# RWKV-7 and forgetting attention on one core: recurrence units of two chunks of four head pairs, and a gate made by a dense stream

## The chip, the cores and the metric

One core of one Trainium2 chip runs the whole forward pass as one program. The metric is the time of that program on the device in microseconds (us). The engines are TensorE (PE in the profile; PEld is its weight load), VectorE (DVE), ScalarE (ACT), GpSimd (POOL) and SyncE (SP), which here issues all DMAs.

## What is computed

A trunk of two layers over 1024 tokens of width 1024, 16 heads of 64, all float32. The first layer is RWKV-7 time mixing, the second forgetting attention; each is followed by a squared-ReLU MLP. The change touches time mixing only:

```python
xr, xw, xk, xv, xa, xg = (h + xx * mu[j] for j in range(6))
r, k, v = xr @ wr, xk @ wk, xv @ wv
w_log = -softplus(-(w0 + tanh(xw @ w1) @ w2)) - 0.5
a = sigmoid(a0 + (xa @ a1) @ a2)
g = sigmoid(xg @ g1) @ g2                      # (T,160) @ (160,1024)
...
sa = einsum('bhvk,bhk->bhv', S, a_t)           # one step of the state, head by head
S = S * w_t[:, :, None, :] + sa[..., :, None] * b_t[..., None, :] + v_t[..., :, None] * k_t[..., None, :]
y = einsum('bhvk,bhk->bhv', S, r_t)
...
y = groupnorm(y) * ln_w + ln_b + bonus
x = x + (1 + gate) * ((y * g) @ wo)
```

## The kernel before

**Chunks and units.** The recurrence is done in chunks of 64 tokens. Two heads lie on the 128 partitions and make a head pair; there are 8 pairs (p in the code) and 16 chunks. A unit (u, 16 of them) is two pairs by four chunks, 256 tokens of one half of the sequence (j): `where(u)` names them, units 0 to 7 are the first half. For each unit `early` makes the decays, scales keys and queries (`ar`, `bk`), and inverts 16x16 blocks on VectorE (L772, L773, through DRAM `Ld`, `T16d`); `late` makes the in-chunk products (`sc`, `xk`, `tt`, `uv`, `bkt`); `chain` carries the state; `gate` normalises the result, multiplies it by the gate and stores it to `yd`.

**A step of the chain.** For each chunk c: state times `ar` into the PSUM tile `pq`, and the state's part of the read-out into `py` (both by `both`, L875); VectorE adds (`xs`, L892); `tt` times `xs` (L875); ScalarE and VectorE copy it into `uv` (L898, L899); for each pair `bkt` times `uv` (L906) and VectorE's state update (L910), GpSimd having scaled the old state (`sp`, L867); and the rest of the read-out (L915). `pq` is one PSUM bank with one buffer. Each `yield` of `chain` ends an inner step, three a chunk.

**What sets the order.** `units` writes the chain's steps at high priority; after each, `step` takes a number of pieces from three other generators in NR rounds: the preparation of later units (PR a step), the gate of the last unit (NG, or NG8 in unit 8), and `beside`, the dense stream (NA, NC or NB a step by the unit). `issue_after` holds these behind the step's instructions, and a scheduler then fixes each engine's order. A piece of the dense stream is one weight tile's share of three f32r matmuls of 128x512 (`mm3`, L124, L126, L128: high by high, low input by high weight, high input by low weight). The dense stream is: the rest of the first half's `v`, then the second half's low-rank projections, `r`, `k`, `v` and the gate's first product (`lora_g`), then, once eight units are gated (`ngated`), the output projection and the MLP of the first half. Ahead of the units, `rest` drains the first half's `r` and `lora_g` beside `early` of units 0 and 1, and `done` takes N0 pieces of `v`.

**The gate.** `lora_g` stores 128 of the 160 sigmoid rows to `gad` in DRAM and keeps 32 in `zt`. `gate` loads them and, for each of the unit's two pairs, the two parts of `g2`, and makes the gate by two fp32 matmuls of 256 columns (L943, L944) into one PSUM tile, by which VectorE multiplies (L946). In the trace an fp32 matmul is two instructions.

## Time and profile before

| what | us |
|---|---|
| median of three runs (3390.83 to 3399.28) | 3394.84 |
| the profiled execution | 3394.05 |
| its span, first to last instruction | 3392.1 |
| opening, to the first state matmul | about 333 |
| recurrence, to the last state matmul | about 1304 |

The profile is of one execution. Busy times are sums over an engine's instructions; a matmul's listed duration includes its way through the array, so consecutive ones overlap and a share near 100% doesn't say how closely they follow each other. A window is a stretch of the span; a wait is idle time of an engine put down to what ended it. In a timeline the first number is the start, and the spacing of starts is what one instruction takes of the queue's time.

### The profile page before, as it was taken

The page shows a single profiled execution, that of the slowest core. Times are in us where ns is not written, and L with a number is a line of the kernel's source. Part 1 is how long each engine was busy: PE and PEld are TensorE (multiplying, and loading weights), DVE is VectorE, ACT ScalarE, POOL GpSimd, SP SyncE. Part 2 cuts the span into 40 slices and gives each one's busy share as a digit, 9 for nine tenths or more (in the row PEclk, how much of TensorE's full clock was granted, in tenths as well). Part 3 has the DMA queues.
Part 4 walks back from the last instruction along what each step waited for, and adds up shares of the span by engine and source line. Part 5 has one row for each costly group of instructions (what it writes and reads, how often), then busy time and mean ns, then how long its engine had stood idle before and what let it go on. Part 6 is the DMA issues. An engine that isn't in the chain of part 4 may idle for free.

```text
span 3392.1 us, 50350 instructions
## 1 busy us (share of the span) xinstructions
PE 3214.4 (95%) x19108; PEld 2438.4 (72%) x19108; DVE 1943.0 (57%) x3239; ACT 1432.8 (42%) x2284; POOL 1358.7 (40%) x868
## 2 busy tenths in 40 slices
PE   4898999999999999899999999999999999999997
PEld 2456666666777776678887777777778888778886
DVE  7496765766556534167786433555566666454344
ACT  3642236523433223242233556667555544332323
POOL 3364432333333233354444432444423333454444
PEclk7899999899999999899999999999999999999999
DMA  7374344355333223236752233666544443232222
GB/s 276 98 234 151 95 128 135 116 152 150 88 102 102 85 76 125 68 111 224 229 187 88 85 131 119 207 203 182 177 128 136 144 134 100 88 111 95 98 98 83
DMA packets 294065, 452.90 MB, mean 134 GB/s; under 512 B 114720, under 2 KB 170432, under 8 KB 293824
## 3 DMA queue, kind: packets, MB, share of 16 engines
q1 hardware_dynamic: 293824, 449.68, 42.3%
q8 instruction: 152, 2.49, 0.3%
q14 instruction: 89, 0.73, 0.1%
HBM read 371.25 MB, written 78.32 MB: 133 GB/s over the span
## 4 chain that ended last, share of the span: by engine, by line
PE 50%; DVE 4%; ACT 2%; DMA 1%; issue 1%; POOL 1%; SPq 0%; DVEq 0%; ACTq 0%; POOLq 0%
PE pj L124 8%; PE pj L128 7%; PE pj L126 7%; PE pk L128 7%; PE pk L124 7%; PE pk L126 7%; PE pt L1328 2%; PE po L1313 1%; PE po L1314 1%; PE ps L1285 1%; PE ps L1286 1%; DVE t L239 1%; DVE hl L241 1%; DVE x L1016 1%; DVE modacc L185 0%
## 5 line engine op out<-in xcount | busy, mean ns | idle before, releaser
L117 POOL TENSOR_TENSOR wl<-wraw,wh 128x1024 fp32r<-128x1024 f32 x385 | 947.7, 2462 | 1231.7 <-ACT wh L116 1162.6
L116 ACT CAST wh<-wraw 128x1024 fp32r<-128x1024 f32 x385 | 402.6, 1046 | 822.0 <-PE pk L126 359.2
L124 PE MATMUL pj<-hh,wh 128*128 128x512 f32 x1120 | 448.6, 408 | 7.4 <-DVE sq L1090 2.7
L128 PE MATMUL pj<-hh,wl 128*128 128x512 f32 x1120 | 445.1, 403 | 5.5 <-POOL wl L117 5.5
L126 PE MATMUL pj<-hl,wh 128*128 128x512 f32 x1120 | 443.2, 401 | 0.0
L1016 DVE SCALAR_TENSOR_TENSOR x<-pj,G,x 128x512 f32<-128x512 f32 x304 | 225.8, 747 | 164.3 <-PE pj L128 162.2
L128 PE MATMUL pk<-hh,wl 128*128 128x512 f32 x688 | 272.1, 402 | 8.6 <-POOL wl L117 8.6
L124 PE MATMUL pk<-hh,wh 128*128 128x512 f32 x688 | 270.2, 398 | 8.9 <-ACT wh L116 7.8
L126 PE MATMUL pk<-hl,wh 128*128 128x512 f32 x688 | 267.3, 395 | 0.0
L124 PEld LDWEIGHTS pj<-hh,wh 128*128 128x128 f32 x1120 | 210.9, 189 | 61.9 <-issue 4.5
L1016 DVE SCALAR_TENSOR_TENSOR x<-pk,G,x 128x512 f32<-128x512 f32 x240 | 176.2, 746 | 135.7 <-PE pk L128 135.2
L128 PEld LDWEIGHTS pj<-hh,wl 128*128 128x128 f32 x1120 | 210.6, 188 | 58.9 <-POOL wl L117 7.7
L126 PEld LDWEIGHTS pj<-hl,wh 128*128 128x128 f32 x1120 | 211.1, 189 | 48.1 <-issue 2.4
L124 PE MATMUL pj<-mh,wh 128*128 128x512 f32 x564 | 236.9, 421 | 6.0 <-DVE mr L1046 3.0
L126 PE MATMUL pj<-ml,wh 128*128 128x512 f32 x564 | 224.3, 398 | 0.0
L128 PE MATMUL pj<-mh,wl 128*128 128x512 f32 x564 | 219.4, 399 | 2.4 <-POOL wl L117 2.4
L124 PE MATMUL pk<-mh,wh 128*128 128x512 f32 x460 | 182.1, 398 | 8.9 <-DVE mr L1046 5.4
L166 ACT CAST mh<-mr 128x512 fp32r<-128x512 f32 x128 | 79.5, 621 | 250.6 <-PE pj L128 109.1
L126 PE MATMUL pk<-ml,wh 128*128 128x512 f32 x460 | 181.7, 395 | 0.0
L185 DVE SCALAR_TENSOR_TENSOR modacc<-modw,cact,modacc 128x1024 f32<-128x1024 f32 x98 | 155.1, 1583 | 31.0 <-DMA modw<-in_modw_dram 22.5
L128 PE MATMUL pk<-mh,wl 128*128 128x512 f32 x460 | 166.6, 397 | 0.0
L124 PEld LDWEIGHTS pk<-hh,wh 128*128 128x128 f32 x688 | 130.7, 190 | 42.8 <-ACT wh L116 11.6
(334 smaller groups left out, 6493.2 us busy)
## 6 DMA issues: line engine op xcount, KB each, us to landing
wraw<-in_up_dram SPq DMA_DIRECT2D x128, 512.0 KB
wraw<-in_down_dram SPq DMA_DIRECT2D x128, 512.0 KB
modw<-in_modw_dram SPq DMA_DIRECT2D x96, 512.0 KB
wraw<-in_wqg_dram SPq DMA_DIRECT2D x32, 512.0 KB
wraw<-in_wk_dram SPq DMA_DIRECT2D x24, 512.0 KB
wraw<-in_wv_dram SPq DMA_DIRECT2D x24, 512.0 KB
x<-in_xT_dram SPq DMA_DIRECT2D x32, 256.0 KB
wraw<-in_wr_dram SPq DMA_DIRECT2D x16, 512.0 KB
```

Of the source, the lines that this page charges most:

```text
L116: nc.scalar.copy(out=wh, in_=raw)
L117: self.weng.tensor_tensor(out=wl, in0=raw, in1=wh.bitcast(F32), op=ALU.subtract)
L124: mm(out=p, lhsT=wh, rhs=hh[k], start=first, stop=False)
L126: mm(out=p, lhsT=wh, rhs=hl[k], start=False, stop=False)
L128: mm(out=p, lhsT=wl, rhs=hh[k], start=False, stop=last)
L166: self.nc.scalar.copy(out=out_h, in_=src)
L185: nc.vector.scalar_tensor_tensor(out=acc, in0=w, scalar=ck, in1=acc, op0=ALU.mult, op1=ALU.add)
L239: nc.vector.scalar_tensor_tensor(out=t, in0=x[k], scalar=A[:, k:k + 1], in1=rs, op0=ALU.mult, op1=ALU.mult)
L241: nc.vector.scalar_tensor_tensor(out=hl[k], in0=t, scalar=sh[:, k:k + 1], in1=hh[k].bitcast(F32), op0=ALU.add, op1=ALU.subtract)
L1016: self.nc.vector.scalar_tensor_tensor(out=x[j][m], in0=ps, scalar=gain[:, m:m + 1], in1=x[j][m], op0=ALU.mult, op1=ALU.add)
L1285: PE.matmul(out=o[:, 0:r], lhsT=qs[:, q], rhs=kh[:, i * n:i * n + r], start=True, stop=False)
L1328: PE.transpose(out=pt[:, i * 256 + b * 128:i * 256 + (b + 1) * 128], in_=Ps[b][:, (k + i) * 128:(k + i + 1) * 128], identity=ident)
```

## The change

A unit becomes four pairs by two chunks (128 tokens). Each inner step so works on four pairs, and there are half as many; the numbers of pieces a step are about doubled (NR 8, NA 5, NC 6, NB 10.8, PR 3.6, NG 4, NG8 1.6). The state tiles are 128x256 instead of 128x128, the decay takes four matmuls of 128 columns instead of two of 256, and loads that go by pair are four instead of two. The state matmuls of a chunk are held behind the preceding read-out's, and the read-out's rest behind the state update's. `x2` reuses `x1`'s memory. `lora_g` now stores all 160 rows; a new generator `gates` reads a half's rows back, splits them and `g2` into high and low parts, and makes the gate for all 8 pairs by dense f32r matmuls: three with K of 128 and one with K of 96 that carries the three products of the 32-row remainder. The result goes to DRAM (`gd`); `gate` loads its part, and GpSimd multiplies. `gates` stands in the dense stream, for the first half at its head, for the second at the end. The second half's `v` runs beside `lora_g`. The opening takes 33 pieces of `r` and of `v` where it took 17.

```diff
-    N0 = 17
-    NR = 4
+    N0 = 33
+    NR = 8
-    NA = 2.2
+    NA = 5
-    NB = 5.4
-    NC = 3
+    NB = 10.8
+    NC = 6
-    PR = 2.2
-    NG = 2
+    PR = 3.6
+    NG = 4
...
         def dense():
+            yield from self.gates(0, ev)
             yield from v
             yield from self.lora_wa(h, 1, lw, al)
-            for i in (1, 2, 0):
+            for i in (1, 2):
                 yield from self.stream(h, 1, i, xj, ev, al)
-            yield from self.lora_g(h, 1, lw)
+            yield from self.both(self.lora_g(h, 1, lw), self.stream(h, 1, 0, xj, ev, al), 2)
+            yield from self.gates(1, ev)
...
+    def gates(self, j, ev):
+        nc, S, V = self.nc, self.nc.scalar, self.nc.vector
+        s = slice(j * HT, (j + 1) * HT)
+        f = lambda n, d=F32R, b=1: ev.tile([128, HT], d, name=n, tag=n, bufs=b)
+        gh, gl, gr = f("e2"), f("e3"), f("e1", F32R, 2)
+        g, r = self.t(), self.t()
+        nc.sync.dma_start(out=g, in_=self.gad[0:128, s])
+        self.split(gh, gl, g)
+        nc.sync.dma_start(out=r[0:32], in_=self.gad[128:160, s])
+        S.copy(out=gr[0:32], in_=r[0:32])
+        S.copy(out=gr[64:96], in_=r[0:32])
+        V.tensor_tensor(out=gr[32:64], in0=r[0:32], in1=gr[0:32].bitcast(F32), op=ALU.subtract)
+        wh, wl = self.load_w(self.ap["g2"][:, 0:128].rearrange("m k n -> k m n"))
...
+        for m in range(KT):
+            p = self.bank()
+            self.mm3([p], wh[:, m], wl[:, m], [(j, [gh], [gl])], 0, True, False)
+            nc.tensor.matmul(out=p, lhsT=wr[0:96, m], rhs=gr[0:96], start=False, stop=True)
+            yield
+            o = f("e0", F32, 2)
+            S.copy(out=o, in_=p)
+            nc.sync.dma_start(out=self.gd[m][:, s], in_=o)
...
         C = 8
+        Q, N = 4, 2
-            j, g, q = u // 8, u % 8 // 2, u % 2
-            return j, 2 * g, slice(j * HT + q * 256, j * HT + (q + 1) * 256)
+            j, g, q = u // 8, u % 8 // 4, u % 4
+            return j, Q * g, slice(j * HT + q * 128, j * HT + (q + 1) * 128)
...
-            for c in range(4):
+            for c in range(N):
...
-                    for q in range(2):
-                        ins = both(ps[:, q], ar[:, 0, q * 4 + c], st[:, q], True, True)
+                    with ExitStack() as ea:
+                        if ins is not None:
+                            ea.enter_context(tc.issue_after(ins.ins))
+                        for q in range(Q):
+                            ins = both(ps[:, q], ar[:, 0, q * N + c], st[:, q], True, True)
...
-                for q in range(2):
-                    for e in range(2):
-                        ins = PE.matmul(out=ys[q][H[e]], lhsT=uv[:, q * 4 + c, e], rhs=sc[:, q * 4 + c, e, 1], start=first and q == 0, stop=c + q == 4)
+                with tc.issue_after(ins.ins):
+                    for q in range(Q):
+                        for e in range(2):
+                            ins = PE.matmul(out=ys[q][H[e]], lhsT=uv[:, q * N + c, e], rhs=sc[:, q * N + c, e, 1], start=first and q == 0, stop=c == N - 1 and q == Q - 1)
...
-            ga = lng("ga", [128, 256], 1)
-            nc.sync.dma_start(out=ga, in_=self.gad[:, ts])
+            g = lng("g", [128, W], 1)
+            nc.sync.dma_start(out=two(g), in_=pair(self.gd, p, ts))
...
-                PE.matmul(out=ps[:, c], lhsT=g2[:, 0], rhs=ga, start=True, stop=False)
-                PE.matmul(out=ps[:, c], lhsT=g2[96:128, 1], rhs=self.zt[96:128, ts], start=False, stop=True)
-                yield
-            V.tensor_tensor(out=y, in0=y, in1=ps, op=ALU.mult)
+            yield
+            G.tensor_tensor(out=y, in0=y, in1=g, op=ALU.mult)
```

How this stands on TensorE, in the order that the program fixes. In these rows `pj` with `wh` or `wl` is a dense matmul, and a count xn is of matmuls as written.

Before, in unit 1: a chain block, one piece of the gate (L943, L944) and dense work.

```order
L906 MATMUL pq<-uv,bkt 64x64
L875 MATMUL py<-ar,st 64x64
L906 MATMUL pq<-uv,bkt 64x64
L875 MATMUL py<-ar,st 64x64
L943 MATMUL pms<-ga,g_2999 128x256
L944 MATMUL pms<-zt,g_2999 128x256
L715 MATMUL pe<-ar,bk 64x64 x8
L126 MATMUL pj<-xl,wh 128x512
L128 MATMUL pj<-xh,wl 128x512
L124 MATMUL pj<-xh,wh 128x512
L126 MATMUL pj<-xl,wh 128x512
L128 MATMUL pj<-xh,wl 128x512
```

State update (L906) and read-out (L875) alternate one by one, and the gate's two fp32 matmuls follow on the same queue.

After, in unit 8: the gate's columns of the second half (`e` is the split gate input, L614 the matmul with K of 96) between preparation and state updates of two matmuls.

```order
L944 MATMUL pq<-uv,bkt 64x64 x2
L749 MATMUL pl<-dT_2018,x_6966 64x64
L614 MATMUL pj<-e_6937,wh 128x512 x2
L749 MATMUL pl<-ta,lb 32x32 x16
L944 MATMUL pq<-uv,bkt 64x64 x2
L124 MATMUL pj<-e_6935,wh 128x512
L126 MATMUL pj<-e_6936,wh 128x512
L128 MATMUL pj<-e_6935,wl 128x512
L614 MATMUL pj<-e_6937,wh 128x512
L124 MATMUL pj<-e_6935,wh 128x512
L126 MATMUL pj<-e_6936,wh 128x512
L128 MATMUL pj<-e_6935,wl 128x512
```

The gate of all pairs is now dense work; the fp32 gate matmuls stand nowhere.

After, in unit 8, some 40 rows on: the end of its first chunk and the first two steps of its second.

```order
L833 MATMUL pl<-ar,bk 128x128 x4
L944 MATMUL pq<-uv,bkt 64x64 x4
L954 MATMUL py<-sc,uv 64x64 x8
L909 MATMUL py<-ar,st 64x64 x6
L749 MATMUL pe<-ar,bk 64x64
L909 MATMUL pq<-st,ar 64x64 x8
L909 MATMUL py<-ar,st 64x64 x2
L749 MATMUL pe<-ar,bk 64x64 x15
L124 MATMUL pj<-hh,wh 128x512
L909 MATMUL pq<-xs,tt 64x64 x8
L126 MATMUL pj<-hl,wh 128x512
```

The read-out and the state products stand in blocks of six to eight matmuls; from the last gate column to the `hh` matmul (the output projection's first) there is no dense work in this step.

Before, the first state matmul of all (L875, `pq<-sc,tt`) and the rows ahead of it, dense matmuls of the stream `v`:

```order
L126 MATMUL pj<-xl,wh 128x512
L128 MATMUL pj<-xh,wl 128x512
L124 MATMUL pj<-xh,wh 128x512
L126 MATMUL pj<-xl,wh 128x512
L128 MATMUL pj<-xh,wl 128x512
L875 MATMUL pq<-sc,tt 64x64 x4
L604 MATMUL pms<-cs,e_2280 128x128 x4
```

After, the same place:

```order
L749 MATMUL pl<-tt,x_2231 32x32 x16
L871 MATMUL pl<-sg,cs 128x512
L124 MATMUL pj<-e_2055,wh 128x512
L126 MATMUL pj<-e_2056,wh 128x512
L128 MATMUL pj<-e_2055,wl 128x512
L614 MATMUL pj<-e_2057,wh 128x512
L909 MATMUL pq<-sc,tt 64x64 x8
L880 MATMUL pl<-cs,bk 128x128 x4
```

The dense matmuls ahead of it are now the gate's of the first half. In all 570 dense matmuls stood ahead of the first state matmul, and now 520, 16 of them the gate's.

## Rows read from the trace of the kernel before

**Rows 1.** The page's part 1, whole execution: busy us (share) xinstructions.

```profile
PE 3214.4 (95%) x19108; PEld 2438.4 (72%) x19108; DVE 1943.0 (57%) x3239; ACT 1432.8 (42%) x2284; POOL 1358.7 (40%) x868
```

**Rows 2.** Windows: stretch, length, busy us (xinstructions) by engine, granted clock, DMA share, GB/s.

```profile
0.00:330.00 330.00, 253.85 (x1093) 157.67 (x1094) 225.97 (x297) 135.99 (x187) 154.38 (x111) 0.84 0.57 189
330.00:1304.00 974.00, 949.33 (x8626) 664.94 (x8626) 572.28 (x1273) 361.05 (x563) 335.57 (x269) 0.98 0.38 112
```

**Rows 3.** Waits of TensorE, 330 to 1304 us: total us, times, longest.

```profile
PE pj L126 <- DVE xl L167: 8.0, 4, 4.5
PE pq L875 <- DVE st L910: 3.9, 2, 2.9
PE pj L124 <- DVE x L1016: 2.9, 4, 1.5
```

**Rows 4.** Windows: a stretch of unit 10 without dense matmuls.

```profile
884.00:897.00 13.00, 9.28 (x162) 6.86 (x158) 6.77 (x15) 5.60 (x9) 2.21 (x3) 0.84 0.33 98
```

**Rows 5.** Timeline of TensorE: start us, us, line, operation; a gate piece in unit 1.

```profile
438.39 0.70 PE L943 MATMUL pms<-ga,g 128*128 128x256 f32 x2
439.02 0.69 PE L944 MATMUL pms<-zt,g 32*128 32x256 f32 x2
439.64 0.49 PE L799 MATMUL pl<-ar,bk 64*128 64x128 f32 x2
440.06 0.50 PE L124 MATMUL pj<-xh,wh 128*128 128x512 f32 x1
440.39 0.40 PE L126 MATMUL pj<-xl,wh 128*128 128x512 f32 x1
```

**Rows 6.** Timeline of TensorE: ten dense matmuls, then a short block.

```profile
424.67 0.39 PE L126 MATMUL pj<-xl,wh 128*128 128x512 f32 x1
...
427.00 0.40 PE L128 MATMUL pj<-xh,wl 128*128 128x512 f32 x1
427.32 0.33 PE L915 MATMUL py<-sc,uv 128*64 128x64 f32 x2
```

**Rows 7.** Timeline of TensorE: chain blocks, in fours, woven, and alternating.

```profile
431.08 0.34 PE L906 MATMUL pq<-uv,bkt 128*64 128x64 f32 x4
431.35 0.50 PE L128 MATMUL pj<-xh,wl 128*128 128x512 f32 x1
...
436.35 0.27 PE L915 MATMUL py<-sc,uv 128*64 128x64 f32 x1
436.36 0.27 PE L906 MATMUL pq<-uv,bkt 128*64 128x64 f32 x1
...
436.86 0.50 PE L124 MATMUL pj<-xh,wh 128*128 128x512 f32 x1
...
440.95 0.33 PE L906 MATMUL pq<-uv,bkt 128*64 128x64 f32 x2
441.21 0.33 PE L875 MATMUL py<-ar,st 64*64 64x64 f32 x2
441.46 0.33 PE L906 MATMUL pq<-uv,bkt 128*64 128x64 f32 x2
```

**Rows 8.** Timeline of TensorE: transposes, then the decay matmuls of a unit.

```profile
431.69 1.03 PE L846 MATMUL pl<-cs,bk 128*128 128x128 f32 x8
432.65 0.45 PE L875 MATMUL pq<-sc,tt 64*64 64x64 f32 x8
433.03 1.13 PE L737 MATMUL pe<-zt,w 65*128 65x256 f32 x4
434.00 1.02 PE L931 MATMUL pms<-t,blk_m 128*128 128x512 f32 x2
```

**Rows 9.** Windows: the end of the opening.

```profile
170.00:285.00 115.00, 98.06 (x414) 63.48 (x414) 108.00 (x129) 42.63 (x62) 74.53 (x44) 0.91 0.63 208
285.00:333.00 48.00, 47.60 (x388) 36.12 (x388) 20.24 (x51) 10.34 (x16) 15.20 (x11) 0.96 0.50 148
```

**Rows 10.** Groups of VectorE, 330 to 1304 us: busy us, mean ns, idle before.

```profile
L910 DVE SCALAR_TENSOR_TENSOR st<-pq,pc,sp 128x64 f32<-128x64 f32 x88 | 24.6, 279 | 46.3 <-PE pq L906 45.6
```

More of the change, by code (lines that the diff above doesn't have):

```diff
@@ L372, in run @@
                 self.take(m1, 100)
-                rs = self.rs = [xq.tile([128, HT], F32, name=f"rs{j}") for j in range(2)]
+                rs = self.rs = [xq1.tile([128, HT], F32, name=f"rs{j}") for j in range(2)]
                 self.rms(x[0], rs[0])
@@ L524, in phase_rwkv @@
         else:
-            self.take(r, 17)
+            self.take(r, 33)
         v = self.stream(h, 0, 0, xj, ev, al)
@@ L585, in lora_g @@
-        nc.sync.dma_start(out=self.gad[:, s], in_=g)
+        for p, o, n in ((ps[0], 0, 128), (ps[1], 128, 32)):
+            g = self.t()
+            S.activation(out=g[0:n], in_=p[0:n], func=AF.Tanh, scale=0.5)
+            nc.gpsimd.tensor_scalar(out=g[0:n], in0=g[0:n], scalar1=0.5, scalar2=0.5, op0=ALU.mult, op1=ALU.add)
+            nc.sync.dma_start(out=self.gad[o:o + n, s], in_=g[0:n])
+    def gates(self, j, ev):
[11 more added lines that the diff above has]
+        wh, wl = self.load_w(self.ap["g2"][:, 0:128].rearrange("m k n -> k m n"))
+        raw, wr = (self.wp.tile([128, KT, 128], d, name=n, tag=n, bufs=b) for n, d, b in (("wraw", F32, self.NW[0]), ("wh", F32R, self.NW[1])))
+        for i in range(3):
+            nc.sync.dma_start(out=raw[i * 32:(i + 1) * 32], in_=self.ap["g2"][:, 128:160].rearrange("m k n -> k m n"))
+        S.copy(out=wr[0:96], in_=raw[0:96])
+        self.weng.tensor_tensor(out=wr[64:96], in0=raw[64:96], in1=wr[64:96].bitcast(F32), op=ALU.subtract)
+        for m in range(KT):
[6 more added lines that the diff above has]
+            nc.sync.dma_start(out=self.gd[m][:, s], in_=o)
@@ L735, in early @@
             ps = bank("pe")
-            for q in range(2):
-                PE.matmul(out=ps[:, q * 256:(q + 1) * 256], lhsT=w2[:, q], rhs=self.zt[0:65, ts], start=True, stop=True)
+            for q in range(Q):
+                PE.matmul(out=ps[:, q * 128:(q + 1) * 128], lhsT=w2[:, q], rhs=self.zt[0:65, ts], start=True, stop=True)
             yield
@@ L753, in early @@
             kr = erl("sg", [128, W], self.SG)
-            for i in range(2):
-                q = slice(i * 4, i * 4 + 4)
+            for i in range(Q):
+                q = slice(i * N, i * N + N)
                 V.scalar_tensor_tensor(out=c3(kr)[:, q], in0=bk[:, q, 1], scalar=self.col("rk", p + i), in1=ar[:, 1, q], op0=ALU.mult, op1=ALU.mult)
@@ L790, in late @@
             uv = lng("uv", [128, C, 2, HD])
-            for q in range(2):
-                nc.sync.dma_start(out=uv[64:128, q * 4:(q + 1) * 4], in_=self.Vd[ts, (p + q) * 128:(p + q + 1) * 128].rearrange("(c s) (e d) -> s c e d", s=64, d=HD))
+            for q in range(Q):
+                nc.sync.dma_start(out=uv[64:128, q * N:(q + 1) * N], in_=self.Vd[ts, (p + q) * 128:(p + q + 1) * 128].rearrange("(c s) (e d) -> s c e d", s=64, d=HD))
             sc = lng("sc", [128, C, 2, 2, HD])
@@ L880, in chain @@
             sp = None if begin else scaled(old, 0)
-            for c in range(4):
-                first, last = begin and c == 0, end and c == 3
-                ys = [yp[:, (q * 4 + c) * HD:(q * 4 + c + 1) * HD] for q in range(2)]
+            ins = None
+            for c in range(N):
+                first, last = begin and c == 0, end and c == N - 1
+                ys = [yp[:, (q * N + c) * HD:(q * N + c + 1) * HD] for q in range(Q)]
                 xs = xk[:, :, c]
@@ L895, in chain @@
                 ps = state()
-                for q in range(2):
-                    ins = both(ps[:, q], tt[:, q * 4 + c], xs[:, q], True, True)
+                for q in range(Q):
+                    ins = both(ps[:, q], tt[:, q * N + c], xs[:, q], True, True)
                 S.copy(out=us[0][:, :, c], in_=ps[H[0]])
@@ L902, in chain @@
                     ps = state()
-                    st = small("st", 3) if c < 3 else old
-                    for q in range(2):
+                    st = small("st", 2) if c < N - 1 else old
+                    for q in range(Q):
                         for e in range(2):
-                            PE.matmul(out=ps[H[e], q], lhsT=bkt[:, q * 4 + c, e], rhs=uv[:, q * 4 + c, e], start=True, stop=True)
+                            ins = PE.matmul(out=ps[H[e], q], lhsT=bkt[:, q * N + c, e], rhs=uv[:, q * N + c, e], start=True, stop=True)
                         if first:
```

60 lines of the change are left out of this document (27 added, 33 removed).

## The prediction

> **What bounds the kernel now.** I read the page's busy times first: TensorE is busy 95% of the span, no other engine over 57% [rows 1]. Then the windows by stage, because the change touches two stages only: the opening up to about 330 us, and the recurrence from there to 1304 us. In the recurrence TensorE is busy 949 of 974 us at a granted clock of 0.98, VectorE 572, ScalarE 361, GpSimd 336, the DMA engines 38% [rows 2]. Busy there could still hide slack, so the third view is who TensorE waited for in that stretch: the longest entry is 8.0 us, and the worst wait that belongs to the chain of states is 3.9 us [rows 3]. So in the recurrence TensorE is the bound, and what counts is the time from one matmul's start to the next one's start, not its listed duration (a dense 128x512 matmul lists 0.39 to 0.40 us, and ten of them start from 424.67 to 427.00 us, 0.233 us each [rows 6]). The opening is another matter: from 170 to 285 us VectorE is busy 108 of 115 us, and only from 285 to 333 us is TensorE the full one [rows 9]. What follows after 1304 us is not changed in kind.
>
> The profiled execution took 3394.05 us (span 3392.1 and 1.95 outside it); the median of the three runs is 3394.84, 0.02% off, so sums against the one hold for the other.
>
> **Part by part.**
>
> The fp32 gate matmuls go. A unit made its gate in two pieces, each of two fp32 matmuls (K of 128 and of 32, 256 columns), and each fp32 matmul is two instructions in the trace. From start to start the first pair takes 0.63 us and the second 0.62 [rows 5], 1.25 us a piece. 16 units of two pieces: 32 x 1.25 = 40.0 us, all on TensorE's own queue, so all on the path: -40.0.
>
> The dense gate comes: 16 columns of four matmuls of 128x512 (three of the split product, one with 96 rows for the short remainder) at 0.233 [rows 6]: 64 x 0.233 = +15.0. Here the Trainium skill would have it otherwise. In "TensorE: Matmul & The Clock Gate", section "Back-to-back issue gap", the spacing of an isolated matmul is its columns over 2.4 GHz and 2.5 ns: 109 ns for 256 columns and 216 ns for 512. By that page 128 instructions of the old gate would cost 14.0 us and the 64 new ones 13.8, and this part would be worth nothing, 25 us less than in my sum. The rows of the old gate stand at 0.31 us an instruction, nearly three times that, and they decide for me.
>
> Fewer broken runs. A dense run that is cut by a short block pays on both sides: 0.32 us on its last matmul instead of 0.233 [rows 6], and 0.33 on its first [rows 5], together 0.19 over the plain spacing. In the whole order the dense runs between the first and the last state matmul go from 279 to 258: 21 x 0.19 = -4.0.
>
> Longer chain blocks. Wider steps let eight matmuls stand together where four, or one, stood: in the whole order the chain's rows fall from 596 to 270, and the single ones from 264 to 15. A single matmul (two instructions) that alternates with one of another shape takes 0.25 to 0.26 us, as long as two in a block of four instructions, 0.27 [rows 7]. 97 singles of the read-out and 96 of the state update alternate: 193 x 0.25 = 48 us against 97 x 0.27 = 26, a gain of up to 22. But at 436.35 us the same kinds, woven together, took 0.51 us for twelve instructions [rows 7], which is what a long block takes: a gain of 0. I take -8, nearer to the second, since the woven form is as frequent.
>
> The decay matmuls change from two of 256 columns to four of 128 a unit. Four instructions of the old kind take 0.97 us; eight fp32 instructions of 128 columns (the transposes) 0.96 [rows 8]: 0, at most 2 us either way.
>
> The opening holds less cover. Ahead of the first state matmul the order had 570 dense matmuls and has 520, 16 of them the gate's. VectorE's instructions there stay 300 against 302, and it is VectorE that fills 170 to 285 us [rows 9], so a part of the 50 missing matmuls saves no time there and is only pushed behind. All pushed: 50 x 0.233 = +11.7; all saved in the full stretch from 285 to 333: 0. Between the two, +6.
>
> A dry step. In unit 8 the dense stream waits for the first eight gated units; the new order has all 32 matmuls of the second half's gate before its first inner step, and in the next none but the chain and the preparation. The nearest row is the dry step of unit 10 in the old kernel: 13 us, TensorE busy 9.28 of them, clock 0.84 [rows 4]. That is 3.7 us idle and about 2 us of clock: 0 to +6; I take +4. The old unit 8 was dry of dense work as well, but its fp32 gate projection filled it.
>
> At nothing: VectorE and ScalarE lose half of the chain's small instructions and VectorE the last gate product, but neither bounds here [rows 2]. GpSimd takes that product (16 in all) and is busy 34%. On SP a unit issues four more loads of the keys and two more of the values, and drops five for the gate and takes one: two more, with 38% of the DMA engines used [rows 2]. The two reads of the stored gate input wait for their own stores; behind them on SP stand weight tiles, of which one lasts 24 x 0.233 = 5.6 us on TensorE, with two buffers. If that cover failed, TensorE would stand for one store and one load at each of the two reads.
>
> Sum: -40.0 + 15.0 - 4.0 - 8 + 6 + 4 = -27.0. 3394.05 - 27 = **3367 us**.
>
> With every term at its good end: -40 + 15 - 4 - 22 = -51, 3343; at its bad end -40 + 15 - 4 + 2 + 11.7 + 6 + 4 = -5.3, 3389.
>
> **Rivals.**
>
> Bare hand-offs, the case on the slower side. Each pair's state update on VectorE (0.279 us, 120 before [rows 10] and as many after) must end before the next pair's matmuls go into the same PSUM bank; they now stand four in a row in a chunk instead of two. Bare, one costs its 0.28 and the 0.33 of the matmul before it [rows 7], 0.6 us. Against it: the old kernel has as many and waited 3.9 us for them in all [rows 3], and the new order puts preparation between them. The gain is gone when 45 of 120 are bare (27 / 0.6); with 75 bare it is 3367 + 45 = 3412. Chance 0.10.
>
> The gate's fp32 matmuls cost columns only: what is removed is worth 128 x 0.117 = 15, no more than what comes, because the 0.31 us in the rows is the neighbours' weight loading and moves to them. 3367 + 25 = 3392. This is also what the page's spacing gives. Against it: 32 pieces, and the spacing stands between two instructions of the same pair too. Chance 0.06.
>
> Half the gain pushed away: the opening starts its chain no earlier and the dry step is worse than in unit 10, with no gain from blocks: -40 + 15 - 4 + 11.7 + 6 = -11, 3383. Chance 0.17.
>
> More than the sum: longer blocks at their good end and, in the recurrence, half of the 2% of clock that is missing there [rows 2] (0.02 x 974 = 19 us) back as the waits halve in number: 3343 to 3350. For it: half as many steps; against: the fp32 blocks stay. Chance 0.15.
>
> **How the numbers follow.** My own case, 3355 to 3380, has 0.52. About 0.3% or 10 us is what a measurement of this kernel can tell from no change, so faster means under 3384.7 and slower above 3405. Faster: 0.52 + 0.15 + a third of 0.17, 0.73; the same: the columns-only case, the rest of the half gain and some of the bare hand-offs, 0.16 together with what I can't name; slower: 0.11. The range reaches from 3338, under the good end, to 3398, past the bad end and the columns-only case; left out are the bare hand-offs and little on the lower side.
>
> **What would show it.** Dense gate columns at 0.23 us a matmul, 64 of them; no fp32 matmul of 256 columns at the gate. The recurrence's chain would begin between 320 and 333 us and its end come some 45 us earlier than 1304, with 84 fewer dense matmuls of the other streams done by then (20 us given back behind). Waits of state matmuls for VectorE under 10 us in all; over 40 us in that list would make the first rival true. A first unit's start later than 335 us, or more than 10 us of idle in unit 8, would make the third one true. If the stage is shorter by less than 10 us with the waits as small as before, the price of the fp32 gate was wrong.

## The result, and the profile after

The change makes the kernel slower: 3430.66 us median of four runs against 3395.44 for the kernel before in the same comparison, a ratio of 1.0101 with a 95% interval of 1.0077 to 1.0124. The profiled execution has a span of 3432.6 us. Medians here and below are of fast runs alone: one run of e8 (4172.8 us, granted clock 0.68) and one of the kernel before (13211 us) are left out. I had forecast 3367 and a range of 3338 to 3398, so the time is outside the range, on the other side of no change.

The page's part 1 of the kernel after (busy us, share, instructions), to lay beside [rows 1]:

```profile
PE 3193.9 (93%) x19108; PEld 2444.5 (71%) x19108; DVE 1983.3 (58%) x3261; ACT 1443.1 (42%) x2276; POOL 1370.8 (40%) x858
```

TensorE's busy time fell by 20.5 us while the span grew by 40.5: 61 us of new idle time. Windows of the kernel after (stretch, length, busy us by engine, granted clock, DMA share, GB/s): the three stages, cut at the first and the last matmul into the PSUM tile of the state products (`pq`), and the end of the opening.

```profile
0.00:339.00 339.00, 253.42 (x1054) 157.94 (x1054) 236.45 (x301) 136.03 (x188) 143.28 (x111) 0.82 0.55 182
339.00:1313.00 974.00, 906.24 (x8559) 652.75 (x8558) 582.82 (x1275) 364.92 (x546) 348.85 (x254) 0.93 0.40 118
1313.00:3433.00 2120.00, 2034.26 (x9500) 1633.84 (x9496) 1163.98 (x1687) 942.11 (x1542) 878.68 (x495) 0.98 0.42 134
170.00:285.00 115.00, 99.13 (x420) 65.21 (x420) 103.89 (x137) 38.72 (x56) 62.95 (x43) 0.89 0.61 203
285.00:339.00 54.00, 45.09 (x319) 32.56 (x317) 26.99 (x42) 12.40 (x20) 13.89 (x10) 0.75 0.42 122
```

The old recurrence, cut in the same way, is this row (the 1304 us given ahead is the end of the last read-out matmul, into `py`; the last one into `pq` ends at 1298):

```profile
333.00:1298.00 965.00, 940.33 (x8578) 658.39 (x8576) 568.11 (x1267) 358.85 (x559) 331.11 (x266) 0.98 0.38 112
```

In the recurrence TensorE is busy 34 us less (906.24 against 940.33), as a shorter queue should give. But the stage is 9 us longer: idle time rose from 24.7 to 67.8 us, and the granted clock fell from 0.98 to 0.93. A mean of 0.93 between full speed and half of it means (1 - 0.93) x 2 x 974 = 136 us at 1.2 GHz; with the clock unrounded it is 134, where the old stage had 41. The waits of TensorE in the stage (us in total, times, longest), to lay beside [rows 3]:

```profile
PE pq L944 <- DVE sv L948: 12.9, 5, 5.1
PE pe L749 <- DVE bk L781: 8.5, 4, 3.5
PE pq L944 <- DVE uv L937: 7.4, 5, 3.4
PE pl L833 <- DVE sc L837: 5.0, 3, 2.9
PE pq L944 <- DVE st L946: 3.0, 2, 2.2
PE pq L944 <- DVE st L948: 2.8, 6, 1.1
```

The state matmuls L944 now wait 26.1 us for VectorE (18.7 of them for state updates, 7.4 for `uv`), and the preparation's matmuls (L749, L833) wait too. In the old stage the same matmuls, L906, waited 2.9 us for `uv` and the updates of all but a unit's first chunk:

```profile
PE pq L906 <- DVE uv L899: 1.8, 3, 0.8
PE pq L906 <- DVE st L910: 1.1, 1, 1.1
```

What a wait costs besides itself is seen at 430 us. VectorE, ScalarE, GpSimd and TensorE there, first as windows, then as a timeline (start us, us, engine, line, operation; in brackets the idle time before and what ended it; `...` where rows are left out):

```profile
424.00:430.00 6.00, 6.00 (x38) 4.01 (x37) 3.52 (x7) 3.80 (x6) 0.00 (x0) 1.00 0.38 98
430.00:437.20 7.20, 2.09 (x42) 1.47 (x42) 6.42 (x12) 5.46 (x8) 4.65 (x2) 0.85 0.53 176
437.20:445.30 8.10, 8.10 (x68) 6.27 (x69) 7.71 (x27) 0.00 (x0) 1.94 (x2) 0.50 0.23 62
445.30:450.00 4.70, 4.70 (x36) 3.59 (x35) 1.61 (x8) 1.84 (x3) 0.72 (x1) 1.00 0.58 186
```

```profile
431.09 0.18 DVE L807 TENSOR_TENSOR ti<-ti,tm 64x28 f32<-64x28 f32 x1
...
431.23 4.65 POOL L117 TENSOR_TENSOR wl<-wraw,wh 128x1024 fp32r<-128x1024 f32 x2 [7.43 <-ACT wh L116]
431.30 2.33 DVE L806 TENSOR_TENSOR tm<-lblk,ti 64x39 f32<-64x39 f32 x1
...
433.66 2.27 DVE L807 TENSOR_TENSOR ti<-ti,tm 64x39 f32<-64x39 f32 x1
...
435.96 0.20 DVE L806 TENSOR_TENSOR tm<-lblk,ti 64x48 f32<-64x48 f32 x1
...
436.80 0.27 DVE L948 SCALAR_TENSOR_TENSOR sv<-pq,pc,sp 128x64 f32<-128x64 f32 x1
437.13 0.48 PE L944 MATMUL pq<-uv,bkt 128*64 128x64 f32 x4 [5.11 <-DVE sv L948]
...
442.40 0.63 PE L128 MATMUL pj<-xh,wl 128*128 128x512 f32 x1
442.83 0.63 PE L124 MATMUL pj<-xh,wh 128*128 128x512 f32 x1
```

VectorE's small preparation instruction L806, 0.20 us at 435.96, took 2.33 us while the first of GpSimd's two subtractions L117 ran, and the next one, L807, took 2.27 beside the second. The state update L948 ran behind them on VectorE, and the next pair's matmuls waited for it: TensorE stood for 5.11 us. Then came 8.1 us at a clock of 0.50, in which dense matmuls start 0.43 us apart (442.40, 442.83) instead of 0.233 [rows 6].

Two other places that the prediction named. The dry step of unit 8 is there (811 to 831 us: 3.1 us idle and a clock of 0.66). And of the 16 columns of the dense gate nine ran at the lower clock, as the two kinds below; at full clock they are 0.23 us apart, as forecast.

```profile
811.00:831.00 20.00, 16.94 (x156) 14.04 (x156) 11.25 (x27) 10.19 (x14) 10.96 (x8) 0.66 0.52 146
```

```profile
801.60 0.63 PE L128 MATMUL pj<-e,wl 128*128 128x512 f32 x1
802.03 0.63 PE L614 MATMUL pj<-e,wh 96*128 96x512 f32 x1
...
808.36 0.39 PE L128 MATMUL pj<-e,wl 128*128 128x512 f32 x1
808.59 0.39 PE L614 MATMUL pj<-e,wh 96*128 96x512 f32 x1
```

### The profile page after: what moved, and what is told of

Its sections match the earlier page's. It is cut to its first block, busy times and chain, and to the rows that moved or that the text cites. A ratio compares the mean times of both kernels' runs of the same rounds, so it can differ in the third digit from the quotient of the medians.

```text
span 3432.6 us, 50369 instructions
## 1 busy us (share of the span) xinstructions
PE 3193.9 (93%) x19108; PEld 2444.5 (71%) x19108; DVE 1983.3 (58%) x3261; ACT 1443.1 (42%) x2276; POOL 1370.8 (40%) x858
## 4 chain that ended last, share of the span: by engine, by line
PE 70%; DVE 14%; ACT 5%; DMA 5%; issue 3%; SPq 1%; POOL 1%; DVEq 0%; ACTq 0%; POOLq 0%
PE pj L124 12%; PE pj L126 11%; PE pj L128 11%; PE pk L128 7%; PE pk L124 7%; PE pk L126 7%; PE pt L1361 2%; PE pl L749 2%; DVE modacc L185 1%; DVE t L702 1%; DVE tm L806 1%; DVE ti L807 1%; PE pl L833 1%; PE po L1346 1%; PE po L1347 1%
## 5 line engine op out<-in xcount | busy, mean ns | idle before, releaser
L117 POOL TENSOR_TENSOR wl<-wraw,wh 128x1024 fp32r<-128x1024 f32 x387 | 949.1, 2454 | 1281.3 <-ACT wh L116 1191.0
L128 PE MATMUL pk<-hh,wl 128*128 128x512 f32 (+1 forms) x704 | 271.1, 400 | 7.0 <-POOL wl L117 7.0
L124 PE MATMUL pk<-hh,wh 128*128 128x512 f32 (+1 forms) x704 | 270.0, 397 | 5.4 <-ACT wh L116 3.0
L126 PE MATMUL pk<-hl,wh 128*128 128x512 f32 (+1 forms) x704 | 269.1, 396 | 0.0
L128 PEld LDWEIGHTS pk<-hh,wl 128*128 128x128 f32 (+1 forms) x704 | 131.2, 187 | 42.6 <-POOL wl L117 11.1
```

The costliest lines, as they stand in the source:

```text
L117: self.weng.tensor_tensor(out=wl, in0=raw, in1=wh.bitcast(F32), op=ALU.subtract)
L124: mm(out=p, lhsT=wh, rhs=hh[k], start=first, stop=False)
L126: mm(out=p, lhsT=wh, rhs=hl[k], start=False, stop=False)
L128: mm(out=p, lhsT=wl, rhs=hh[k], start=False, stop=last)
```

## The experiments

One table for all of them. The median is as above, and the stages are those of its one profiled execution, which can lie some us from its median (e5, e7 and e13 by 7). Opening, recurrence and rest are cut at the first and the last matmul into `pq`; "dense" counts the dense matmuls in the stage, "idle" is the recurrence's length less TensorE's busy time in its window, and "other" its length less 0.233 us for each dense matmul, so that stages with more or less of the dense stream can be compared. The median of the kernel before is 3397 to 3399 in the comparisons of the experiments.

| kernel | median | ratio, 95% | opening (dense) | recurrence (dense) | idle | clock | other | rest |
|---|---|---|---|---|---|---|---|---|
| before | 3395.4 | | 333 (570) | 965 (1818) | 24.7 | 0.98 | 541 | 2094 |
| after | 3430.7 | 1.0077 to 1.0124 | 339 (520) | 974 (1854) | 67.8 | 0.93 | 542 | 2120 |
| e1 gates only | 3417.9 | 1.0043 to 1.0080 | 315 (476) | 1013 (1955) | 50.3 | 0.95 | 557 | 2083 |
| e2 units only | 3428.2 | 1.0074 to 1.0108 | 346 (576) | 954 (1720) | 43.9 | 0.93 | 553 | 2127 |
| e3 after, state matmuls first | 3382.7 | 0.9943 to 0.9973 | 342 (520) | 921 (1814) | 67.6 | 0.95 | 498 | 2119 |
| e4 after, update in two | 3378.4 | 0.9917 to 0.9960 | 340 (520) | 918 (1812) | 65.7 | 0.94 | 496 | 2121 |
| e5 units only, state matmuls first | 3428.8 | 1.0081 to 1.0114 | 348 (576) | 947 (1662) | 63.3 | 0.92 | 560 | 2139 |
| e6 before, state matmuls first | 3378.7 | 0.9934 to 0.9964 | 331 (570) | 938 (1764) | 38.0 | 0.96 | 527 | 2110 |
| e7 before, order shifted | 3402.9 | 1.0010 to 1.0032 | 332 (570) | 975 (1797) | 29.2 | 0.97 | 556 | 2101 |
| e8 after, subtraction in halves | 3382.1 | 0.9946 to 0.9978 | 329 (520) | 968 (1854) | 64.6 | 0.94 | 536 | 2082 |
| e9 before, no gate matmuls | 3397.8 | 0.9988 to 1.0014 | 332 (570) | 967 (1818) | 53.9 | 0.96 | 543 | 2093 |
| e10 after, work put back | 3449.3 | 1.0129 to 1.0175 | 337 (520) | 978 (1852) | 66.4 | 0.95 | 547 | 2130 |
| e11 before, subtraction in halves | 3381.9 | 0.9936 to 0.9970 | 331 (570) | 981 (1818) | 36.1 | 0.97 | 557 | 2068 |
| e12 e4 and e8 together | 3340.8 | 0.9803 to 0.9850 | 331 (520) | 920 (1812) | 74.7 | 0.95 | 498 | 2088 |
| e13 after, preparation at 4.4 | 3411.1 | 1.0024 to 1.0052 | 340 (520) | 960 (1843) | 60.7 | 0.93 | 531 | 2116 |
| e14 before, gate matmuls twice | 3440.2 | 1.0103 to 1.0135 | 334 (570) | 1004 (1818) | 24.9 | 0.98 | 580 | 2100 |
| e15 e6 and e11 together | 3358.8 | 0.9864 to 0.9900 | 330 (570) | 945 (1764) | 35.5 | 0.95 | 534 | 2083 |
| e16 e12, preparation at 4.4 | 3344.6 | 0.9824 to 0.9854 | 332 (520) | 920 (1800) | 63.6 | 0.94 | 500 | 2093 |

Six times fit none of the cases that I had set out: e3, e4 and e8 came out below them, e5 above, e2 and e11 between. The others lie within 2 us of one of theirs.

**Theories at the start.** A: the new waits come from state updates that split the state matmuls of a chunk. B: the dense gate is at fault, since the fp32 gate's matmuls had covered waits. C: VectorE's updates are late because GpSimd's long instruction holds it.

**The two parts apart.** e1 is the kernel before with the new `lora_g`, `gates` and `gate` (for two pairs):

```diff
+            yield from self.gates(0, ev)
             yield from v
...
             yield from self.lora_g(h, 1, lw)
+            yield from self.gates(1, ev)
```

e2 is the kernel after with the old `lora_g` and `gate` (for four pairs):

```diff
-            yield from self.gates(0, ev)
             yield from v
...
-            yield from self.gates(1, ev)
```

> The kernel before with the dense gate alone: units of two pairs by four chunks, the old numbers of pieces, NG and opening. If the fp32 gate matmuls were worth 1.25 us a piece and the dense ones 0.233 us each, as I had it, 25 us less than before less a few for the opening: 3368 to 3380. If their price was wrong (they cost only their columns), 3390 to 3400. If the loss of the whole change lies in the gate (its place at the head of the dense stream), 3410 to 3430.

> The changed kernel with the old fp32 gate inside each unit: the wide units and their numbers alone. If the loss lies in the wide units (TensorE waiting for state updates and preparation, and the clock after it), slower than the changed kernel by the gate's worth: 3445 to 3460. If it lies in the dense gate, near before or faster: 3375 to 3395.

Each part alone is slower, by 20.6 and 30.8 us. So neither is the good half of a change that the other one spoils, and the gate's 25 us of my sum do not appear anywhere: the new units with the old gate (e2) take 2.5 us less than with the new one.

**The split update.** e3 is the kernel after with this edit, the four pairs' matmuls ahead of their four updates:

```diff
                     for q in range(Q):
                         for e in range(2):
                             ins = PE.matmul(out=ps[H[e], q], lhsT=bkt[:, q * N + c, e], rhs=uv[:, q * N + c, e], start=True, stop=True)
+                    for q in range(Q):
                         if first:
```

> The changed kernel with all eight state matmuls of a chunk written first and the four updates on VectorE after them, so that TensorE need not wait for one pair's update before the next pair's matmuls. If the bare hand-offs are the cause (19 us of waits between them, and the lower clock behind the waits), 3390 to 3410 and the waits of pq matmuls for VectorE under 12 us. If they are only where a general lack of cover shows, 3420 to 3435 with the waits moved to other matmuls.

e4 also replaces the four updates by one product and one sum over all four pairs:

```diff
-                            ins2 = V.scalar_tensor_tensor(out=st[:, q], in0=ps[:, q], scalar=pc[:, q, c:c + 1], in1=sp[:, q], op0=ALU.mult, op1=ALU.add)
+                    pcb = pc[:, :, c:c + 1].broadcast_to([128, Q, HD])
...
+                        V.tensor_tensor(out=st, in0=ps, in1=pcb, op=ALU.mult)
+                        ins2 = V.tensor_tensor(out=st, in0=st, in1=sp, op=ALU.add)
```

> The changed kernel with the state update of a chunk made by two VectorE instructions over all four pairs instead of four. Removes three hand-offs in four as well, and shortens VectorE's part from 1.1 to about 0.8 us. If the hand-offs are the cause, 3385 to 3410; if not, 3420 to 3435.

Both are 48 to 52 us faster than the change as it is, and faster than the kernel before. The group of the state matmuls in the recurrence (count, busy us, mean ns, idle time before and what ended it), in before, after and e3:

```profile
L906 PE MATMUL pq<-uv,bkt 128*64 128x64 f32 x480 | 59.5, 247 | 3.7 <-DVE uv L899 1.8 <-DVE st L910 1.1 <-DVE st L908 0.3
```

```profile
L944 PE MATMUL pq<-uv,bkt 128*64 128x64 f32 x480 | 43.7, 263 | 28.1 <-DVE sv L948 12.9 <-DVE uv L937 7.4 <-DVE st L946 3.0
```

```profile
L944 PE MATMUL pq<-uv,bkt 128*64 128x64 f32 x480 | 23.2, 234 | 8.5 <-DVE bkt L882 4.0 <-DVE uv L937 2.3 <-DVE ti L807 2.0
```

Busy and idle of this one line go from 71.8 us in after to 31.7 in e3. But the idle time of the stage stays as it was, 67.6 against 67.8 us: other waits took the place of these. What shrank is TensorE's busy time, 906 to 853 us, with 40 dense matmuls fewer (9 us). The window of e3's recurrence:

```profile
342.00:1263.00 921.00, 853.38 (x8518) 629.93 (x8514) 599.06 (x1271) 361.98 (x541) 344.11 (x252) 0.95 0.43 125
```

In e3 sixteen of these instructions stand together and take 0.51 us, from 422.87 to the next block's start:

```profile
422.87 0.69 PE L944 MATMUL pq<-uv,bkt 128*64 128x64 f32 x16
423.38 0.64 PE L955 MATMUL py<-sc,uv 128*64 128x64 f32 x16
```

A block of four costs 0.27 [rows 7], and so a chunk's four blocks 1.1, without what they break up: in the recurrence the blocks of state-update matmuls go from 116 to 37, and the dense runs from 258 to 205. An estimate from these numbers: 120 blocks are 30 chunk steps, at 1.08 - 0.51 = 0.57 us each 17 us; 53 dense runs fewer at 0.19 are 10 us; the dense matmuls that moved on are 9; and the stage spent 35 us less at the lower clock (134 to 99), worth at most half of it, 17. Together that is the 53 us. So A was right about the place, and half wrong about how it is paid: the hand-offs cost by cutting TensorE's queue into short blocks and by the clock, and not by an idle time that goes when they go. e6 is the same edit in the old kernel, which gains 18.8 us:

```diff
                     for q in range(2):
                         for e in range(2):
                             PE.matmul(out=ps[H[e], q], lhsT=bkt[:, q * 4 + c, e], rhs=uv[:, q * 4 + c, e], start=True, stop=True)
+                    for q in range(2):
                         if first:
```

> The kernel before with one change: the state matmuls of both pairs ahead of their two VectorE updates. If it is the hand-off between an update and the next pair's matmuls that costs: only 60 such hand-offs go (90 in the change), with 1.4 us of waits in all, so a gain of 5 to 20 us, 3377 to 3392. If e3's gain of 48 us came from repairing something that only the wide units have: within 5 us of 3397. If longer blocks alone make it (one break of a dense run less each, 0.19 us x 54): 3387.

e5, the same edit on the new units with the old gate, does not tell what I made it for:

> The changed units with the old fp32 gate, and the state matmuls of all four pairs ahead of their four VectorE updates. Against e3 (the same with the dense gate, 3382.66 us) this measures the gate alone, with the hand-offs out of the way. If the gate's 25 us of TensorE time are real and were lost only to waits: 3403 to 3410. If the dense gate is worth nothing, or costs as in e1 (+20): 3362 to 3385.

It is as slow as e2, and its largest wait is one that only this mixture has: the fp32 gate now needs four loads of `g2` a unit through one buffer, and TensorE waits for them (in e2, with the same loads, 3.6 us).

```profile
PE pms L951 <- DMA g<-in_g_dram: 18.1, 8, 5.5
```

So e5 against e3 is no measure of the gate. This is answered by two runs on the old units.

**The gate's matmuls on the old units, taken out and doubled.** e9 leaves out L943 and L944 and puts nothing in their place (the last product then reads the tile of the statistics, and the gate is missing from the result); e14 makes each of them twice. The edit of e9:

```diff
-            ps = self.small()
...
-                PE.matmul(out=ps[:, c], lhsT=g2[:, 0], rhs=ga, start=True, stop=False)
-                PE.matmul(out=ps[:, c], lhsT=g2[96:128, 1], rhs=self.zt[96:128, ts], start=False, stop=True)
```

> The kernel before with the 64 fp32 gate matmuls (128 instructions) left out and nothing in their place; the loads stay, and the last product takes the bank of the statistics instead, so the gate is not computed. This measures the term of -40.0 by itself. If those matmuls stood on the path: 3397 - 40 = 3357. If they covered waits of the chain, and what is taken out comes back as waits and as a lower granted clock: 3377 to 3397.

> The kernel before with the old gate's matmuls made twice (128 more instructions, 40 us more of TensorE's queue; the second pass starts the sum anew, so the values stay). If the old kernel stands at a balance of TensorE's queue and the chain: about +40 in full or a little less, 3425 to 3440. If the chain alone sets the stage, so that the gate's matmuls lie in its waits: 3397 to 3412.

The windows of the recurrence in e9 and in e14, beside the row of before above:

```profile
333.00:1298.00 965.00, 911.12 (x8441) 647.45 (x8440) 573.08 (x1265) 358.75 (x558) 326.41 (x265) 0.96 0.38 112
```

```profile
333.00:1337.00 1004.00, 979.10 (x8700) 674.65 (x8699) 568.95 (x1267) 359.09 (x558) 330.04 (x267) 0.98 0.37 107
```

Doubled, they cost 42.1 us, the whole of their queue time (128 x 0.31 = 40). Taken out, they are worth nothing: 3397.8 against 3398.6. TensorE's busy time falls by 29 us, not by 40, in the same 965 us with the same 1818 dense matmuls, and all of the 29 turn up as idle time. The other 11 fit the clock, which goes to 0.96: unrounded 31 us more at the lower level, which is worth up to 15. Of e9's 54 us of idle time 18 are waits of the state matmuls for VectorE, where before had 2.9 for the same two entries:

```profile
PE pq L906 <- DVE st L910: 12.0, 4, 5.7
PE pj L124 <- DVE x L1013: 9.3, 9, 2.0
PE pq L906 <- DVE uv L899: 6.2, 5, 3.0
```

So the old kernel stood at a balance: added work cost its full price and removed work bought nothing. That is theory B, in a stronger form than I had given it. That the chain of hand-offs to and from the other engines is what is as long as TensorE's queue is my reading of these waits; the chain's own length was not measured. e1 then follows: 0 for what goes, 15 for the dense gate, and 5 that these runs do not place. On the new units e10 puts as many idle fp32 instructions of 256 columns back into `gate`:

```diff
-            yield
+            ps = self.small()
+            for q in range(2):
+                c = slice(q * 256, (q + 1) * 256)
+                PE.matmul(out=ps[:, c], lhsT=self.blk_m, rhs=g[:, c], start=True, stop=False)
+                PE.matmul(out=ps[:, c], lhsT=self.blk_m, rhs=g[:, c], start=False, stop=True)
+                yield
```

> The changed kernel with as much fp32 work put back beside its units as the old gate had (64 matmuls of 128 by 256, 128 instructions, 40 us of TensorE by the old rows), whose result nobody reads. If TensorE's queue is the bound: 3431 + 40 = 3471. If the new units lack cover, so that most of it falls into waits: 3425 to 3450.

It costs 18.6 us, but its price is not the 40 that I had expected. All its instructions have one weight, `blk_m`, and they follow each other faster than the gate's did, as at this place:

```profile
472.22 0.59 PE L981 MATMUL pms<-g,blk_m 128*128 128x256 f32 x2
472.65 0.59 PE L982 MATMUL pms<-g,blk_m 128*128 128x256 f32 x2
472.89 0.58 PE L124 MATMUL pj<-xh,wh 128*128 128x512 f32 x1
473.31 0.39 PE L126 MATMUL pj<-xl,wh 128*128 128x512 f32 x1
```

From 472.22 to 473.31 is 1.09 us, less 0.23 for the dense matmul 0.86 a piece, where a gate piece took 1.25 [rows 5]; 32 pieces are 27 us. So some two thirds of the price were paid. The recurrence grew by 4 us only, and 11 us came behind it. In the recurrence the idle time stayed (66.4 against 67.8 us), TensorE's busy time rose by 5 (911.55 against 906.24), and the clock rose from 0.93 to 0.95, which is 32 us less at the lower level:

```profile
337.00:1315.00 978.00, 911.55 (x8670) 655.57 (x8665) 578.99 (x1274) 366.81 (x546) 346.03 (x254) 0.95 0.41 118
```

So the stage's idle time did not shrink; what the work did not cost in this stage it got back from the clock, at least in part.

**GpSimd's subtraction in halves**, for theory C:

```diff
-        self.weng.tensor_tensor(out=wl, in0=raw, in1=wh.bitcast(F32), op=ALU.subtract)
+        m = shape[1] // 2
+        for a in (slice(0, m), slice(m, shape[1])):
+            self.weng.tensor_tensor(out=wl[:, a], in0=raw[:, a], in1=wh[:, a].bitcast(F32), op=ALU.subtract)
```

> The changed kernel with GpSimd's subtraction for a split weight tile (2.46 us in one instruction) made in two halves. If VectorE's updates come late because VectorE's small instructions are held while that instruction runs (0.19 us became 2.3 us at 431 us), the longest stretches halve and the waits for updates fall from 12.9 + 7.4 us to about half, with some of the clock back: 3405 to 3422. If they come late for the order on VectorE alone: 3428 to 3434.

> The kernel before with GpSimd's subtraction for a split weight tile in two halves, as in e8 (-47 us for the changed kernel, 38 of them after the recurrence). If that gain is one of the stage that both kernels share: 3397 - 35 to - 47, 3350 to 3362. If it only mended what the change did (VectorE's late updates): within 8 us of 3397.

The time looks like a triumph for C, 48.5 us, but the place is another: the recurrence keeps 64.6 us of idle time and is 6 us shorter, the opening is 10 us shorter, and 37 us of the profiled executions' 53 lie behind the recurrence, in a stage that both kernels have. The old kernel gains 16.7 us, 26 behind the recurrence and 15 of that lost in it, which these runs do not explain. Yet with the subtraction in halves the two kernels take the same time, 3382.1 and 3381.9 us, and the loss of 35 us is gone. By this measure C takes away as much as A, whose edit leaves 3382.7 (e3) against 3378.7 (e6). So C explains waits like the one at 431 us, and cannot be ruled out as a part of the loss; each of the two repairs alone removes nearly all of it, and the runs do not share it out between them. Waits for the subtraction's result behind the recurrence, in after and in e8, and the windows of that stage in e8, before and e11:

```profile
PE pk L128 <- POOL wl L117: 9.2, 9, 2.3
```

```profile
PE pk L130 <- POOL wl L119: 2.0, 5, 0.7
```

```profile
1297.00:3380.00 2083.00, 2023.41 (x9513) 1630.99 (x9512) 1128.80 (x1688) 942.62 (x1542) 945.26 (x783) 0.99 0.43 136
```

```profile
1298.00:3392.00 2094.00, 2017.20 (x9426) 1620.11 (x9426) 1147.33 (x1674) 937.97 (x1538) 870.96 (x491) 0.99 0.42 135
```

```profile
1312.00:3379.00 2067.00, 2004.31 (x9418) 1611.66 (x9416) 1115.45 (x1674) 939.24 (x1537) 931.26 (x775) 0.99 0.43 137
```

VectorE's busy time falls by 35 and 32 us with the same instructions, while GpSimd's rises by 66 and 60.

**Order and rates.** e7 only shifts the old kernel's order, and e13 spreads the new kernel's preparation at twice the old rate:

```diff
-    PR = 2.2
+    PR = 2.4
```

```diff
-    PR = 3.6
+    PR = 4.4
```

> A control: the kernel before with the same instructions, but the preparation spread at a rate of 2.4 in place of 2.2, so that only the order shifts. If the time hangs on how the order happens to fall (a tuned order against any other), this costs 10 to 25 us, 3407 to 3422, with the clock falling from 0.957 to about 0.95; if not, within 6 us of 3397.

> The changed kernel with its preparation spread at 4.4 a step instead of 3.6 (twice the old 2.2, as the steps are half as many). If the waits come from preparation that is left over and stands without dense work beside it: its 46 us of waits in stretches of over 5 us without a dense matmul fall to 25 or less, 3400 to 3415. If the rate is not it: 3423 to 3440.

A shifted order costs 5.5 us (the old clock, 0.957 in the expectation, is 0.970), so differences of 5 us between kernels of different order are nothing to explain. The rate is worth 19.5 us of the 35 lost, with 7 us less idle time; in stretches of over 5 us without a dense matmul idle falls from 46 to 34 us, not to the 25 that I had asked for. Preparation that is left over is a part of it.

**Both repairs.** e12 is e4 with e8's edit, e15 is e6 with it, and e16 is e12 with e13's rate.

> The changed kernel with the state update of all four pairs as two VectorE instructions (e4, 3378) and GpSimd's subtraction in halves (e8, 3384). If the two act on different stretches: 3378 - 40 = 3338 to 3345. If they mend the same late updates: 3370 to 3380.

> The kernel before with both repairs: the state matmuls of both pairs ahead of their updates (e6, -18.8) and GpSimd's subtraction in halves (e11, -16.9). If the two add: 3397 - 36 = 3361, and the changed kernel with its repairs (e12, 3340.8) keeps 20 us of its own. If the change is worth nothing of itself: 3338 to 3345.

> The version of e12 with the preparation spread at 4.4 a step instead of 3.6. If left-over preparation causes its 82 us of waits in the recurrence: 3315 to 3330. If not: 3335 to 3350.

e12 is the fastest, 3340.8 us, 1.7% under the kernel before; its two edits gave 52 and 49 us apart and give 90 together. The old units with the state matmuls first and the subtraction in halves take 3358.8, 18 us more. The update made by two instructions, which only e12 has, is worth up to 4 of these (e4 against e3). So the change is worth 14 to 18 us of its own once its updates do not split the queue and VectorE is held for less long, half to two thirds of the 27 that I had forecast. The rate adds nothing there.

## Why the prediction was wrong

By stages, with dense matmuls counted at 0.233 us wherever they run, the 40.5 us are: dense gate 64 x 0.233 = 14.9; opening 17.7 (6 us longer with 50 dense matmuls fewer); recurrence 0 (541 and 542 us of other); rest about 7.5 (26 us longer with 78 dense matmuls more). My sum had 15, 6, -48 and 0 for these. The recurrence is what failed.

**The step that failed** is the first term: "all on TensorE's own queue, so all on the path: -40.0". The price was right: e14 measures 42.1 for the same instructions. The worth was 0 in the old units (e9); in the new units the exchange of the old gate for the dense one lost 2.5 us (the change against e2) where my sum has a gain of 25. I had read from [rows 2] that TensorE is the bound, 949 of 974 us busy. That row tells what more work would cost. It does not tell how far behind the next limit lies, and here it lay right behind. I take it to be the chain across TensorE, VectorE, ScalarE and GpSimd, the other three busy for less than 60% of the stage; e9's waits point there, but no run measured the chain by itself. With 25 us of idle time in the stage I took TensorE's queue for the whole of it; I should have asked what a chunk takes by its hand-offs alone.

That the change came out slower and not merely without gain goes with two things that either repair takes away, as above: its split state updates (e3, e4) and VectorE being held beside GpSimd's subtraction (e8).

By the Trainium skill's spacing ("TensorE: Matmul & The Clock Gate", section "Back-to-back issue gap") this part would have been worth nothing, and it was; but for the price the rows hold and that spacing does not. The 128 instructions cost 42 us when added; the 14 worked out from the spacing is an estimate. The rival that rested on that price (3392, columns only) so gave a right worth by a mechanism that e14 refutes.

**The clock.** My sum had 2 us of it, in the dry step. A wait is paid twice here: TensorE stands, and then runs at 1.2 GHz for some us (0.50 from 437.20 to 445.30 us). The recurrence's time at the lower level grew from 41 to 134 us. I had even listed the missing 2% of clock as something to win back.

**Fewer broken runs, longer blocks** (-4, -8): the queue did get shorter. With -40, -4, -8 and 8 for 36 more dense matmuls in the stage, busy time should fall by 44; it fell by 34 at a lower clock, which lengthens it by up to half of the 93 us that came to the lower level, 47 us. These terms cannot be separated further. What I missed in them is that one of the new blocks is no block: the state update stays cut in four (e3, e4).

**Decay matmuls** (0): eight instructions of 128 columns take 0.89 us, from 340.33 to 341.22, where four of 256 took 0.97 [rows 8]. Right.

**Opening** (+6, at most 11.7): 17.7, past my bad end. From 285 to 339 us TensorE is busy 45.09 of 54 us at a clock of 0.75, where it was busy 47.60 of 48 at 0.96 [rows 9]. My bad end assumed that removed cover costs at most its own length. The sign I gave for this, a start later than 335 us, came (339).

**Dry step** (+4): there, 3.1 us idle and a clock of 0.66 over 20 us; the 0.34 that are missing are at most 6.8 us, so 3 to 10.

**Dense gate** (+15): the price at full clock was right; nine of 16 columns at the lower one make it some 36 x 0.19 = 7 us more, an estimate from the two spacings.

**Rest** (nothing): about 7.5 us. Idle time there rose by 9 us, and I can't say more than that. At nothing stood VectorE too, which I had losing instructions: over the whole execution it has 22 more, and its busy time rose by 40 us (1943.0 to 1983.3).

**The rivals.** Bare hand-offs (3412, chance 0.10) named a right place and the right sign. I set it at 10 because the old kernel "has as many and waited 3.9 us for them". The 3.9 was a misreading: that row [rows 3] is the next chunk's state product waiting for an update, and the next pair's matmuls waited 1.1. The new waits of the state matmuls were 26 us, between my marks of 10 and 40; e3 shows that the rest of the price lies in short blocks and the clock, and that taking the waits away there only moves them. The half gain and more than the sum didn't come. Only the columns-only rival had the removed gate at no gain, and by its price; none said what e9 and e14 show, that work of the full price is worth nothing when it is taken out. Two slips in the working change nothing of this: the bad end adds a 4 that no term has, and the five cases' chances add up to 1.00, which leaves nothing for what I couldn't name.

## What to carry to other kernels

A TensorE that is busy for 97% of a stage is a sign that added work costs, not that removed work pays: before the price of removed instructions is counted as a gain, leave them out alone and double them alone, and see both slopes (here 0 and 42 us). In a chain of short matmuls with hand-offs, issue all matmuls of a step before the first vector instruction that reads them; a split step pays in short blocks and broken dense runs besides its waits. When two repairs each remove a loss, try them on both kernels before one is named the cause. And price a stall with the clock that follows it.

## What the runs showed of the hardware

A VectorE instruction can be held for as long as a GpSimd instruction lasts: 0.18 us became 2.33 and 2.27 beside two subtractions of 2.3 us each, and ended within 0.05 us of them. The Trainium skill says so ("SBUF — State Buffer", section "Terms"): the two engines share a port pair that one of them holds for a whole instruction, while the other is blocked; by the Trainium skill's "GPSIMD Engine Reference", section "1. Specifications", it concerns VectorE instructions with two inputs from SBUF, as `tm<-lblk,ti` has, or in a two-port mode. The trace agrees, and e8 and e11 put a number on it: two instructions of half the size instead of one give 32 to 35 us of VectorE's busy time back behind the recurrence, with as many instructions of VectorE. The kernels gain 17 and 49 us by it, though no run shows how much of that comes from VectorE.

The lower level of the clock follows stalls: after a wait of 5.11 us, 8.1 us at 0.50. Of the 19 stretches at 1.2 GHz in the new recurrence 18, with 130 of the 134 us, begin in or shortly behind a wait of TensorE of 0.7 us or more; the one from 1039 to 1043 us has no wait ahead of it. Not each wait is followed by one: of the 27 waits over 1 us in that stage eight, of 1.0 to 1.7 us, are not.

fp32 matmuls of 256 columns took 0.31 us an instruction where two weights alternate (K of 128 and 32, the old gate) and 0.22 where all have one weight (e10, 472.22 to 472.65 us for two).

What stays open: which of the chain's hand-offs takes over when TensorE's queue gets shorter. In e9 a third of the idle time is waits of the state matmuls, but one wait of 2.8 us there (L715 for VectorE's `bk`) is no hand-off of the chain: VectorE had itself waited 4.7 us for a load of `bk` to land, in an order of TensorE's instructions that is the same as in before at that place.
